# One decode-and-prompt step of a hybrid trunk: every fp32 tile at an offset of a table, in another order of the same steps

## The chip, the cores and the metric

The kernel runs on one core of one Trainium2 chip. The metric is the time of one execution on the device, in microseconds. The core's engines are TensorE (PE; its weight loads are shown apart as PEld), VectorE (DVE), ScalarE (ACT), GpSimd (POOL) and SyncE (SP). SP, ACT and POOL also issue transfers between HBM and the on-chip memory.

## The reference

One layer of a trunk with two branches side by side, run on a prompt of 512 tokens and on 8 sequences that each add one token to a past of 4,096.

```python
mod = silu(c) @ w_ada + b_ada;  shift, scale, gate = split(mod, 3)
h = rmsnorm(x, g_norm) * (1 + scale) + shift
q, k, v, z_att, fl, u, z_ssm = split(h @ w_in)     # 512 each, fl: 8
logf = log_sigmoid(fl + b_fgate)
# attention, 8 heads of 64: scores get the sum of logf between the key and the query
#   prompt: causal over 512;  samples: 4096 past rows through page_table, and the new one
# state-space branch: 32 groups of 16 channels, 64 complex states each
#   h_t = a_bar * h_{t-1} + b_bar u_t;  y = Re(C h) + d_skip * u
att = o_att * silu(z_att)
g = gelu(y);  ssm = g * sigmoid(g @ w_glu + b_glu) * silu(z_ssm)
y = x + gate * (concat(att, ssm) @ w_out)          # then a final rmsnorm
```

All is fp32. The outputs are y for prompt and samples, the new k, v and logf, and the last states. The cache that the samples read is 8 x 4096 rows of k and as many of v, 512 values a row: 134 MB, by far the largest part of what is read.

## The kernel before

**Steps and order.** The kernel is written as a program that records. `Engine` wraps each engine, and every call on it (`V.` for DVE, `A.` for ACT, `P.` for POOL, `PE.`, `SP.`) adds one step to a list in `Steps`. There are 2,881 steps; a step can hold several matrix products that go side by side on TensorE (`join`). At the end `issue()` goes through a table `ORDER` of 2,881 step numbers and issues the steps in that order, so that the table fixes the order on each engine's queue. Waits between engines follow from which memory a step reads and writes. All instructions of the profile are therefore issued in one line, L245, and are told apart by their tiles.

**The decode part.** `decode()` walks through 64 blocks of K and 64 of V: 8 for each of 8 sequences. `issue(n)` takes a buffer of 128 x 2048 fp32 (1.05 MB) from `kvt()` and fills it by an indirect gather from POOL's queue, 8 KB a partition. `dec_k(n)` multiplies half of a K block by the query on POOL and half on DVE, and sums over the head dimension, a quarter on ACT (32 short instructions) and the rest by a reduction on DVE. `dec_soft(b)` makes the softmax of a sequence. `dec_v(n)` multiplies a V block on TensorE into the PSUM tile `pv`.

**The prompt part.** `prompt()` holds the rest: the state-space branch `ssm_phase()`, the projections, `attn()` over four pairs of heads and four blocks of 128 queries, the gates, the output projection. Before both, in the body of the function, come the adaLN products, the transposed input `hT`, and the tables of the state-space part, which are a long chain of small DVE steps. The weights come in tiles of 1 MB from SP's queue (`wload`, `w`, `qk`).

**Memory.** Small constants, `hT` and the like have a pool of their own (`cp`). Other tiles come from rings: `wp` has 3 buffers of 1 MB, `qkp` 2, `kva` 3, and `sm` 2 of each name. Two arenas, `arA` (12,864 fp32 a partition) and `arB` (12,640), are single tiles in which `Arena` hands out fixed ranges by name; the memory of the early tables in `arA` is used again later under other names. A cache block has one of five buffers, three of the ring `kva` and two in `arA`:

```python
def kvt():
    n = kvp[0]
    kvp[0] += 1
    if kvp[1] is not None and n % 5 in (1, 2):
        return kvp[1].tile([128, 2048], F32, name="kv", bufs=2)
    return kva.tile([128, 2048], F32, name="kv")
```

PSUM's eight banks are rings too: three for products (`mm`), two for transposes (`tr`), and one each for `sm`, `pv` and `q`.

In the profile `kv` is a buffer of the ring and `arA` can be a cache block, a table or anything else of that arena.

Of the kernel before, what the change touches and what calls it, by code (L numbers as in the profile page):

```python
# [21 lines left out]
B = 8  # L22
# [10 lines left out]
AK = 50.25  # L33
BK = 49.375
# [24 lines left out]
ORDER = [  # L59
# [1462 lines left out]
```

## Time and profile before

| what | value |
|---|---|
| median of three runs | 576.67 us (571.11 to 577.95) |
| profiled execution | 576.52 us, span 574.5 us |
| mean granted TensorE clock | 0.948 |
| moved | 176.50 MB, mean 307 GB/s |
| of this, gathers from POOL (queue q0) | 135.74 MB |
| PE busy | 471.2 us, 82% of the span |
| DVE busy | 405.3 us, 71% |
| POOL busy | 315.4 us, 55% |
| ACT busy | 288.4 us, 50% |

The span goes from the first instruction to the last. A busy share is that of an engine over the span or a part of it; PE's is modelled and is not a share of its peak. The row of the transfers gives the mean busy share of 16 transfer engines. A row of waits reads: who waited, for whom, us in total, how often, the longest. A row of a group reads: line, engine, operation, what is written from what, count, busy us, mean ns of one, and the idle time before them with what ended it. A row of the chain reads: start, us, what.

### The profile page before, as it was taken

Reading aid. Unit: us, or ns where it says so; the run is one execution under the profiler, and the core shown is the slowest. Engines: PE = TensorE matmul, PEld = TensorE weight load, DVE = VectorE, ACT = ScalarE, POOL = GpSimd, SP = SyncE. Lnnn points to the kernel's source line nnn. Section 1 sums busy time; section 2 is a strip of 40 time slices with the busy share of each in tenths; the row PEclk is TensorE's granted clock in tenths of the full one; section 3 lists DMA queues with packets and bytes.
Section 4 is the critical chain, followed back from the end, with each engine's and each line's share of the span. In section 5 each row is a group of like instructions: output and inputs, shape, how many; then the busy total and the mean of one; then the engine's idle time right before and its main releaser. Section 6 shows DMA issues by size and latency. Waiting matters only on the chain.

```text
span 574.5 us, 9192 instructions
## 1 busy us (share of the span) xinstructions
PE 471.2 (82%) x3158; PEld 227.6 (40%) x3158; DVE 405.3 (71%) x712; ACT 288.4 (50%) x1353; POOL 315.4 (55%) x239
## 2 busy tenths in 40 slices
PE   1847795899798987789997988789789799989984
PEld 1315384455343435455532332333234343433331
DVE  6998999989988776455586466676664662765535
ACT  4344252435236834616354895687874782532211
POOL 6157174445168757665636566547845664536431
PEclk9969899799799999999998998999899889999998
DMA  8979544564498999999998898999999899699883
GB/s 252 385 259 290 193 150 147 192 251 136 158 338 334 339 354 356 335 357 370 329 372 295 318 354 315 411 374 327 352 364 362 317 371 413 246 374 349 344 359 149
DMA packets 45335, 176.50 MB, mean 307 GB/s; under 512 B 6981, under 2 KB 21737, under 8 KB 27881
## 3 DMA queue, kind: packets, MB, share of 16 engines
q0 software_dynamic: 19264, 135.74, 63.1%
q1 hardware_dynamic: 25376, 39.40, 19.6%
q10 hardware_dynamic: 648, 0.78, 0.4%
q8 instruction: 25, 0.41, 0.3%
q14 instruction: 22, 0.17, 0.1%
HBM read 171.48 MB, written 4.42 MB: 306 GB/s over the span
## 4 chain that ended last, share of the span: by engine, by line
DMA 35%; DVE 18%; PE 13%; issue 11%; POOL 8%; ACT 5%; POOLq 0%; DVEq 0%; ACTq 0%
DMA kv<-in_cache_k_dram,kidx 16%; PE mm L245 9%; DMA kv<-in_cache_v_dram,kidx 7%; DVE arA L245 6%; DMA arA<-in_cache_v_dram,kidx 6%; POOL kv L245 5%; DVE sc L245 5%; DMA arA<-in_cache_k_dram,kidx 4%; PE pv L245 3%; DVE kv L245 3%; POOL arA L245 3%; ACT arB L245 2%; DVE arB L245 2%; ACT kv L245 1%; DVE hT L245 1%
## 5 line engine op out<-in xcount | busy, mean ns | idle before, releaser
L245 PE MATMUL mm<-hT,w 128*128 128x512 f32 x256 | 130.1, 631 | 1.3 <-PE pv L245 0.6
L245 ACT ACTIVATE kv<-kv 128x64 f32<-128x64 f32 x304 | 73.7, 244 | 68.0 <-DVE kv L245 58.7
L245 POOL TENSOR_TENSOR kv<-kv,qs 128x1024 f32<-128x1024 f32 x38 | 89.7, 2363 | 30.7 <-DMA kv<-in_cache_k_dram,kidx 29.7
L245 ACT ACTIVATE arA<-arA 128x64 f32<-128x64 f32 (+1 forms) x215 | 52.4, 246 | 50.4 <-DVE arA L245 47.9
L245 POOL TENSOR_TENSOR arA<-arA,qs 128x1024 f32<-128x1024 f32 x26 | 61.6, 2369 | 28.1 <-DMA arA<-in_cache_k_dram,kidx 22.4
L245 DVE TENSOR_TENSOR kv<-kv,q 128x1024 f32<-128x1024 f32 x38 | 46.0, 1213 | 35.0 <-DMA kv<-in_cache_k_dram,kidx 28.1
L245 POOL DMA_INDIRECT kv<-in_cache_k_dram,kidx x38 | 37.6, 988 | 58.7 <-PE pv L245 13.3
L245 DVE TENSOR_REDUCE sc<-kv 128x24 f32<-128x1536 f32 x38 | 66.2, 1743 | 3.6 <-POOL kv L245 3.4
L245 PEld LDWEIGHTS mm<-hT,w 128*128 128x128 f32 x256 | 45.7, 198 | 47.6 <-issue 42.9
L245 POOL DMA_INDIRECT kv<-in_cache_v_dram,kidx x38 | 37.7, 992 | 42.3 <-PE pv L245 20.2
L245 ACT ACTIVATION_READ_ACCUMULATOR kv<-kv 128x1 f32 x304 | 57.5, 189 | 0.0
L245 DVE TENSOR_TENSOR arA<-arA,q 128x1024 f32<-128x1024 f32 x26 | 31.5, 1213 | 34.9 <-DMA arA<-in_cache_k_dram,kidx 31.3
L245 PE MATMUL pv<-kv,arA 128*32 128x512 f32 x304 | 42.0, 630 | 16.9 <-DMA kv<-in_cache_v_dram,kidx 16.5
L245 DVE TENSOR_REDUCE sc<-arA 128x24 f32<-128x1536 f32 x26 | 45.4, 1745 | 6.1 <-POOL arA L245 5.9
L245 DVE TENSOR_TENSOR arA<-arA 128x512 f32<-128x512 f32 (+9 forms) x105 | 45.2, 452 | 0.8
L245 POOL DMA_INDIRECT arA<-in_cache_k_dram,kidx x26 | 25.2, 969 | 37.4 <-PE pv L245 25.5
L245 ACT ACTIVATION_READ_ACCUMULATOR arA<-arA 128x1 f32 x208 | 39.4, 189 | 0.0
L245 PE MATMUL mm<-qk,hT 128*64 128x256 f32 x256 | 32.9, 419 | 7.2 <-ACT arA L245 7.0
L245 PE MATMUL pv<-arA 128*32 128x512 f32 x208 | 28.5, 623 | 11.2 <-DMA arA<-in_cache_v_dram,kidx 8.3
L245 POOL DMA_INDIRECT arA<-in_cache_v_dram,kidx x26 | 25.3, 975 | 18.6 <-ACT arA L245 7.6
L245 ACT ACT_TABLE_LOAD x25 | 32.1, 1283 | 4.3 <-PEq L1504 1.7
L245 PEld LDWEIGHTS mm<-qk,hT 128*64 128x64 f32 x256 | 26.1, 201 | 12.9 <-ACT arA L245 7.4
(245 smaller groups left out, 835.1 us busy)
## 6 DMA issues: line engine op xcount, KB each, us to landing
w<-in_w_in_dram SPq DMA_DIRECT2D x10, 1024.0 KB
w<-in_w_ada_dram SPq DMA_DIRECT2D x9, 1024.0 KB
kv<-in_x_prompt_dram SPq DMA_DIRECT2D x2, 1024.0 KB
qk<-in_w_ada_dram SPq DMA_DIRECT2D x2, 1024.0 KB
qk<-in_w_in_dram SPq DMA_DIRECT2D x2, 1024.0 KB
qk<-in_w_out_dram SPq DMA_DIRECT2D x2, 1024.0 KB
w<-in_w_out_dram SPq DMA_DIRECT2D x2, 1024.0 KB
hT<-in_x_prompt_dram SPq DMA_DIRECT2D x1, 2048.0 KB
```

What stands on the lines that cost most here:

```text
L245: fn(*args, **kw)
```

## The change

The rings and arenas go. There is one block, `heap`, of 51,712 fp32 a partition, and eight PSUM tiles, one for each bank. A second table, `PLACE`, has one entry for each of the 671 fp32 and PSUM tiles in the order in which the program asks for them: an offset in the block, or a bank. Tiles of other types (bf16 and int32) get memory of their own. `ORDER` is another permutation of the same 2,881 step numbers. `kvt()` no longer has five buffers but a place from the table for each of the 128 blocks. The table `Toep`, which lay over the memory of `slotB`, gets an entry of its own.

```diff
-AK = 50.25
-BK = 49.375
+HEAP = 51712
+ORDER = [
+    201, 336, 50, 22, 21, 4, 112, 39, 64, 23, 24, 43, 37, 38, 42, 484, 135, 11, 276, 1, 25, 202, 41, 5, 3, 182,
...
-ORDER = [
-    4, 337, 1711, 25, 23, 24, 242, 1, 202, 3, 201, 50, 484, 336, 21, 22, 60, 64, 39, 112, 41, 6, 243, 11, 61,
...
-class Ring:
-    def __init__(self, pool, bufs):
-        self.pool, self.bufs = pool, bufs
-
-    def tile(self, shape, dtype, name, bufs=None):
-        return self.pool.tile(shape, dtype, name=name, bufs=bufs or self.bufs)
...
+    def tile(self, shape, name, psum=False):
+        at, w = PLACE[self.n], int(np.prod(shape[1:]))
+        self.n += 1
+        v = self.banks[at][:shape[0], 0:w] if psum else self.heap[:shape[0], at:at + w]
...
-class Arena:
...
-    cp, sm, wp, qkp, kva = (ring(n, b) for n, b in (("consts", 1), ("small", 2), ("w", 3), ("qk", 2), ("kva", 3)))
-    ps = ring("ps", 1, space=PSUM)
-    ar = ctx.enter_context(tc.tile_pool(name="arenas", bufs=1))
-    arA = ar.tile([128, int(AK * 256)], F32, name="arA")
-    arB = ar.tile([128, int(BK * 256)], F32, name="arB")
...
+    heap = cp.tile([128, HEAP], F32, name="heap")
+    banks = [pp.tile([128, 512], F32, name=f"bank{i}") for i in range(8)]
...
+    class Room:
+        def tile(self, shape, dtype, name, bufs=1, room=0):
+            return T_(shape, name) if dtype == F32 else fixed(shape, dtype, name + str(steps.n))
+
+    cp_, sm, wp, qkp, kva, sa, tb, tp = (Room() for _ in range(8))
+
+    mmt = trt = tbt = smt = bank
...
     def kvt():
         n = kvp[0]
         kvp[0] += 1
-        if kvp[1] is not None and n % 5 in (1, 2):
-            return kvp[1].tile([128, 2048], F32, name="kv", bufs=2)
         return kva.tile([128, 2048], F32, name="kv")
...
-        o = tp.names["slotB0"][0]
-        Toep = arB[:, o:o + 4096].rearrange("p (a j x) -> p a j x", a=2, j=4)
+        Toep = T_([128, 2, 4, 512], "Toep")
...
         if b % 4 == 0 and c == 0:
-            pv_t[0] = ps.tile([128, 512], F32, name="pv", bufs=1)
+            pv_t[0] = bank()
```

More of the change, by code (lines that the diff above doesn't have):

```diff
@@ L32 @@
 PRE = 1
-AK = 50.25
-BK = 49.375
+HEAP = 51712
+ORDER = [
[151 rows of a table added]
+PLACE = [
[36 rows of a table added]
 XAT = 5
@@ L53, with __init__, own, add @@
 NEG = -1e30
-ORDER = [
[151 rows of a table removed]
-]
 class Engine:
     def __init__(self, steps, name, eng):
-        self._s, self._e = steps, eng
+        self._s, self._n, self._e = steps, name, eng
     def __getattr__(self, method):
-        return lambda *args, join=False, **kw: self._s.add(getattr(self._e, method), args, kw, join)
-class Ring:
-    def __init__(self, pool, bufs):
-        self.pool, self.bufs = pool, bufs
-    def tile(self, shape, dtype, name, bufs=None):
-        return self.pool.tile(shape, dtype, name=name, bufs=bufs or self.bufs)
-class Steps:
-    def __init__(self):
-        self.ops = []
-    def add(self, fn, args, kw, join):
+        return lambda *args, join=False, **kw: self._s.add(self._n, method, getattr(self._e, method), args, kw, join)
+class Steps:
+    def __init__(self, nc, heap, banks):
+        self.ops, self.heap, self.banks, self.n = [], heap, banks, 0
+    def tile(self, shape, name, psum=False):
+        at, w = PLACE[self.n], int(np.prod(shape[1:]))
+        self.n += 1
+        v = self.banks[at][:shape[0], 0:w] if psum else self.heap[:shape[0], at:at + w]
+        if len(shape) > 2:
+            ax = "abcd"[:len(shape) - 1]
+            v = v.rearrange(f"p ({' '.join(ax)}) -> p {' '.join(ax)}", **dict(zip(ax, shape[1:])))
+        return v
+    def own(self, t):
+        return t
+    def add(self, eng, method, fn, args, kw, join):
         if join:
@@ L245, in issue @@
                 fn(*args, **kw)
-class Arena:
-    def __init__(self, t, start=0):
-        self.t, self.at, self.names = t, start, {}
-    def tile(self, shape, dtype, name, bufs=1, room=0):
-        n = max(room, int(np.prod(shape[1:])))
-        if name not in self.names:
-            self.names[name] = [self.at, n, bufs, 0]
-            self.at += n * bufs
-            assert self.at <= self.t.shape[1], (name, self.at)
-        e = self.names[name]
-        assert n <= e[1], name
-        o = e[0] + e[1] * (e[3] % e[2])
-        v = self.t[:shape[0], o:o + int(np.prod(shape[1:]))]
-        e[3] += 1
-        if len(shape) > 2:
-            ax = "abcd"[:len(shape) - 1]
-            v = v.rearrange(f"p ({' '.join(ax)}) -> p {' '.join(ax)}", **dict(zip(ax, shape[1:])))
-        return v
 def dap(t, off, dims):
@@ L281, in tile_fox_s5_step, with T_, bank, fixed @@
     ctx.enter_context(tc.manual_schedule())
-    plan = Steps()
-    V, A, P, PE, SP = (Engine(plan, n, e) for n, e in (("DVE", nc.vector), ("ACT", nc.scalar), ("Pool", nc.gpsimd),
-                                                       ("PE", nc.tensor), ("SP", nc.sync)))
-    def ring(name, bufs, **k):
-        return Ring(ctx.enter_context(tc.tile_pool(name=name, bufs=bufs, **k)), bufs)
-    cp, sm, wp, qkp, kva = (ring(n, b) for n, b in (("consts", 1), ("small", 2), ("w", 3), ("qk", 2), ("kva", 3)))
-    ps = ring("ps", 1, space=PSUM)
-    ar = ctx.enter_context(tc.tile_pool(name="arenas", bufs=1))
-    arA = ar.tile([128, int(AK * 256)], F32, name="arA")
-    arB = ar.tile([128, int(BK * 256)], F32, name="arB")
-    sa = tb = Arena(arA)
-    tp = Arena(arB)
-    def mmt():
-        return ps.tile([128, 512], F32, name="mm", bufs=3)
-    def trt():
-        return ps.tile([128, 512], F32, name="tr", bufs=2)
-    tbn = [0]
-    def tbt():
-        tbn[0] += 1
-        return ps.tile([128, 512], F32, name=("sm", "pv")[tbn[0] % 2], bufs=1)
-    def smt():
-        return ps.tile([128, 512], F32, name="sm", bufs=1)
+    cp = ctx.enter_context(tc.tile_pool(name="consts", bufs=1))
+    pp = ctx.enter_context(tc.tile_pool(name="banks", bufs=1, space=PSUM))
+    heap = cp.tile([128, HEAP], F32, name="heap")
+    banks = [pp.tile([128, 512], F32, name=f"bank{i}") for i in range(8)]
+    steps = Steps(nc, heap, banks)
+    V, A, P, PE, SP = (Engine(steps, n, e) for n, e in (("DVE", nc.vector), ("ACT", nc.scalar), ("Pool", nc.gpsimd),
+                                                        ("PE", nc.tensor), ("SP", nc.sync)))
+    def T_(shape, name):
+        return steps.tile(shape, name)
+    def bank():
+        return steps.tile([128, 512], "bank", psum=True)
+    def fixed(shape, dtype, name):
+        return steps.own(cp.tile(shape, dtype, name=name))
+    class Room:
[3 more added lines that the diff above has]
+    mmt = trt = tbt = smt = bank
     def mm(out, lhsT, rhs, start=True, stop=True, **k):
@@ L365, in tile_fox_s5_step @@
         wada.append(t)
-    pt_i = cp.tile([NPG, B], I32, name="pt_i")
+    pt_i = cp_.tile([NPG, B], I32, name="pt_i")
     P.dma_start(pt_i, dap(page_table, 0, [[1, NPG], [NPG, B]]))
-    ident = cp.tile([128, 128], F32, name="ident")
+    ident = cp_.tile([128, 128], F32, name="ident")
     pcol = sa.tile([128, 1], F32, name="pcol")
     P.iota(pcol, pattern=[[1, 1]], base=0, channel_multiplier=1, allow_small_or_imprecise_dtypes=True)
-    ones = cp.tile([128, 128], F32, name="ones")
+    ones = cp_.tile([128, 128], F32, name="ones")
     V.memset(ones, 1.0)
@@ L379, in tile_fox_s5_step @@
         bns.append(bn)
-    bfr = cp.tile([8, 8], F32, name="bfr")
+    bfr = cp_.tile([8, 8], F32, name="bfr")
     P.dma_start(bfr, dap(b_fgate, 0, [[0, 8], [1, 8]]))
-    bfc = cp.tile([8, 1], F32, name="bfc")
+    bfc = cp_.tile([8, 1], F32, name="bfc")
     P.dma_start(bfc, dap(b_fgate, 0, [[1, 8], [1, 1]]))
@@ L393, in tile_fox_s5_step @@
     P.affine_select(tri, ones, pattern=[[-1, 128]], compare_op=OP.is_gt, fill=0.0, base=0, channel_multiplier=1)
-    identb = cp.tile([128, 128], BF16, name="identb")
+    identb = cp_.tile([128, 128], BF16, name="identb")
     V.tensor_copy(identb, ident)
-    maskb = cp.tile([128, 128], BF16, name="maskb")
+    maskb = cp_.tile([128, 128], BF16, name="maskb")
     P.memset(maskb, 0.0)
     P.affine_select(maskb, maskb, pattern=[[-1, 128]], compare_op=OP.is_ge, fill=NEG, base=0, channel_multiplier=1)
-    nhalf = cp.tile([128, 8], F32, name="nhalf")
+    nhalf = cp_.tile([128, 8], F32, name="nhalf")
     V.memset(nhalf, -0.5)
-    s4 = cp.tile([128, 32], F32, name="s4")
+    s4 = cp_.tile([128, 32], F32, name="s4")
     V.tensor_reduce(s4, ident.rearrange("p (q x) -> p x q", x=32), axis=AX.X, op=OP.add)
-    m8c = cp.tile([128, 8], F32, name="m8c")
+    m8c = cp_.tile([128, 8], F32, name="m8c")
     V.tensor_reduce(m8c, ident.rearrange("p (q h) -> p h q", h=8), axis=AX.X, op=OP.add)
-    oh = cp.tile([128, 2, 8], F32, name="oh")
+    oh = cp_.tile([128, 2, 8], F32, name="oh")
     V.memset(oh, 0.0)
@@ L415, in tile_fox_s5_step @@
     PE.transpose(t[:, 128:192], xs64, ident[:64, :64])
-    cs = cp.tile([128, 8, 32], F32, name="cs")
+    cs = cp_.tile([128, 8, 32], F32, name="cs")
     V.memset(cs, 0.0)
     A.activation(cs[:, :, 0:9], t[:, 0:72].rearrange("p (r k) -> p k r", k=8), AF.Silu)
-    gcol = cp.tile([128, 12], F32, name="gcol")
+    gcol = cp_.tile([128, 12], F32, name="gcol")
     V.tensor_copy(gcol, t[:, 72:84])
@@ L459, in tile_fox_s5_step @@
     V.tensor_scalar(rowf, pg4[:, :B], pm, None, op0=OP.add)
-    lidx = cp.tile([128, B], I32, name="lidx")
+    lidx = cp_.tile([128, B], I32, name="lidx")
     V.tensor_copy(lidx, rowf)
-    kidx = cp.tile([128, B, 8], I32, name="kidx")
+    kidx = cp_.tile([128, B, 8], I32, name="kidx")
     for c in range(8):
@@ L472, in gather @@
                                     in_offset=bass.IndirectOffsetOnAxis(ap=idx, axis=0))
-    suf = cp.tile([128, B, 33, H], F32, name="suf")
+    suf = cp_.tile([128, B, 33, H], F32, name="suf")
     for b in range(B):
         gather(suf[:, b, 0:32].rearrange("p s h -> p (s h)"), lrows, lidx[:, b:b + 1])
-    hT = cp.tile([128, 8, S], F32, name="hT")
+    hT = cp_.tile([128, 8, S], F32, name="hT")
     ssx = tb.tile([128, 4], F32, name="ssx")
@@ L509, in tile_fox_s5_step @@
     V.scalar_tensor_tensor(Am, Am, 1.0, gcol[:, 0:8, None].to_broadcast([128, 8, 9]), op0=OP.add, op1=OP.mult)
-    hTs = cp.tile([128, 8, 32], F32, name="hTs")
+    hTs = cp_.tile([128, 8, 32], F32, name="hTs")
     V.memset(hTs, 0.0)
@@ L547, in svec @@
     def svec(name, pool=None):
-        return (pool or cp).tile([8, 512], F32, name=name)
-    xq = cp.tile([128, 512], F32, name="q_s")
+        return (pool or cp_).tile([8, 512], F32, name=name)
+    xq = cp_.tile([128, 512], F32, name="q_s")
     xs2 = xq[:, 0:256]
@@ L557, in tile_fox_s5_step @@
             acopy(q_s[:, c], t, scale=HD ** -0.5)
-    s4b = cp.tile([128, 32], BF16, name="s4b")
+    s4b = cp_.tile([128, 32], BF16, name="s4b")
     V.tensor_copy(s4b, s4)
-    qsp = cp.tile([72, 512], BF16, name="qsp")
+    qsp = cp_.tile([72, 512], BF16, name="qsp")
     V.memset(qsp, 0.0)
@@ L797, in dec_q @@
     def dec_q(b):
-        dq = ps.tile([128, 512], F32, name="q", bufs=1)
+        dq = bank()
         mm(dq, s4b[:72, b:b + 1].to_broadcast([72, 128]), qsp)
@@ L826, in tile_fox_s5_step @@
     V.tensor_copy(xf[:, 0:32], t[:, 0:32])
-    lf = cp.tile([128, 40], F32, name="lf")
+    lf = cp_.tile([128, 40], F32, name="lf")
     z1 = tb.tile([128, 40], F32, name="z1")
@@ L856, in suffix @@
             V.tensor_tensor(suf[:, :, s], suf[:, :, s], suf[:, :, s + 1], op=OP.add)
-    mT = cp.tile([8, 8], F32, name="mT")
-    sn = cp.tile([8, 8], F32, name="sn")
-    den = cp.tile([128, B, H], F32, name="den")
+    mT = cp_.tile([8, 8], F32, name="mT")
+    sn = cp_.tile([8, 8], F32, name="sn")
+    den = cp_.tile([128, B, H], F32, name="den")
     pv_t = [None]
@@ L1057, in attn @@
         attT = res["attT"]
-        spare = Arena(arA, kvp[1].names["gr"][0])
-        cum = spare.tile([8, S], F32, name="cum")
+        cum = T_([8, S], "cum")
         t = trt()
@@ L1063, in attn @@
         V.tensor_tensor_scan(cum, ones[:8, 0:1].to_broadcast([8, S]), t[:8], 0.0, op0=OP.mult, op1=OP.subtract)
-        ncs = cp.tile([72, S], BF16, name="ncs")
+        ncs = cp_.tile([72, S], BF16, name="ncs")
         V.memset(ncs, 0.0)
@@ L1267, in sample_kv @@
             A.dma_start(xs2[32 * j:32 * j + 8], dap(x_sample, 256 * j, [[D, 8], [1, 256]]))
-    late = Arena(arA)
+    late = Room()
     kvp[1] = m8p[0] = m8p[1] = late
@@ L1299, in prompt @@
         yield from fill
-        rp = ap = Arena(arB)
+        rp = ap = Room()
         v_sv, za_s = u_s, y_sv
@@ L1391, in prompt @@
         drain(at)
-        ap = Arena(arB, rp.names["PT0"][0])
         wo = []
@@ L1458, in tile_fox_s5_step @@
         next(gp)
-    acc, steps = 0, 0
+    acc, turns = 0, 0
     while True:
-        acc += R1 if steps < N1 else RATE
-        steps += 1
+        acc += R1 if turns < N1 else RATE
+        turns += 1
         while acc >= 1:
@@ L1489, in tile_fox_s5_step @@
         (SP, A)[j % 2].dma_start(dap(y_s, 256 * j, [[D, 8], [1, 256]]), xs2[32 * j:32 * j + 8])
-    plan.issue()
+    steps.issue()
 _INS = ["x_prompt", "x_sample", "c_prompt", "c_sample", "cache_k", "cache_v", "cache_logf",
```

336 rows, old and new, of tables (ORDER, PLACE) are left out of this document.

## The prediction

> **What bounds the kernel now.** The page's totals come first, then its strip of 40 slices, then the same strip cut into four stages.
>
> ```profile
> span 574.5 us, 9192 instructions
> PE 471.2 (82%) x3158; PEld 227.6 (40%) x3158; DVE 405.3 (71%) x712; ACT 288.4 (50%) x1353; POOL 315.4 (55%) x239
> ...
> DMA  8979544564498999999998898999999899699883
> ...
> q0 software_dynamic: 19264, 135.74, 63.1%
> q1 hardware_dynamic: 25376, 39.40, 19.6%
> ```
>
> No engine is full over the span. The strip shows two regimes: transfers at 4 to 6 tenths from the fifth to the eleventh slice, then 8 to 9 tenths nearly to the end. q0 carries the gathers of the cache, 128 of 1.05 MB (8 KB in each of 128 partitions), and they are most of the traffic.
>
> ```profile
> core 0: us, PE busy (x) PEld busy (x) DVE busy (x) ACT busy (x) POOL busy (x), PEclk, DMA share, GB/s
> 0.00:57.40 57.40, 30.32 (x282) 15.92 (x283) 49.76 (x164) 23.32 (x37) 30.14 (x34) 0.91 0.89 297
> 57.40:172.30 114.90, 98.24 (x784) 57.93 (x788) 109.19 (x236) 44.89 (x251) 52.47 (x35) 0.91 0.55 195
> 172.30:545.70 373.40, 323.58 (x1969) 146.39 (x1962) 233.30 (x286) 216.18 (x1057) 225.82 (x159) 0.97 0.93 347
> 545.70:574.50 28.80, 19.02 (x133) 7.40 (x131) 13.05 (x28) 4.05 (x9) 6.92 (x12) 0.92 0.63 254
> ```
>
> In the first stage the weights come in and transfers are nearly full. In the second, DVE is busy for 109.19 of 114.90 us (the tables of the state-space part and the first score products) and the transfers are idle for 45% of the time, 52 us. In the third, 373.40 us long, transfers are at 0.93 and every engine has room: DVE 140 us, PE 49.8, POOL 147.6. The last is the end of the work, where little is left to move.
>
> The chain that ended last says what the third stage waits for.
>
> ```profile
> DMA 35%; DVE 18%; PE 13%; issue 11%; POOL 8%; ACT 5%; POOLq 0%; DVEq 0%; ACTq 0%
> ```
> ```profile
> 182.38 1.22 issue
> 183.60 7.56 DMA kv<-in_cache_k_dram,kidx
> 191.30 2.36 POOL kv L245
> 193.66 0.89 POOL arA L245
> 194.54 1.85 issue
> 196.62 1.04 POOL kv L245
> 197.96 7.49 DMA kv<-in_cache_k_dram,kidx
> 205.59 2.35 POOL kv L245
> ```
>
> This is a loop through POOL's queue. A gather takes some 7.5 us to land; a product on POOL (2.36 us) waits for it; only when that is done does POOL come to its next gather, and the loop starts again. The waits of the third stage tell the same from both sides.
>
> ```profile
> POOL kv L245 <- DMA kv<-in_cache_k_dram,kidx: 29.7, 16, 5.4
> POOL kv L245 <- PE pv L245: 26.0, 11, 4.6
> POOL arA L245 <- DMA arA<-in_cache_k_dram,kidx: 16.8, 8, 4.5
> POOL arA L245 <- PE pv L245: 16.6, 11, 3.7
> POOL kv L245 <- ACT kv L245: 13.4, 9, 4.2
> ...
> POOL arA L245 <- ACT arA L245: 7.6, 4, 3.9
> ```
> ```profile
> PE pv L245 <- DMA kv<-in_cache_v_dram,kidx: 16.5, 11, 3.9
> ...
> PE pv L245 <- DMA arA<-in_cache_v_dram,kidx: 6.8, 8, 1.7
> ```
>
> POOL's products wait 46.5 us for transfers; its gathers wait 63.6 us (35 times, 1.8 us each) until PE or ACT has finished with the buffer that they will fill. PE waits 23.3 us for V blocks. So the third stage is bound by the **transfers, at a depth that five buffers allow**: 7% of 373 us, 26 us, are idle although data is wanted.
>
> **The change, part by part.**
>
> *Allocators replaced.* Both ORDER tables hold the same 2,881 step numbers, so no instruction is added or taken and shapes stay. The classes that go run at build time: 0 us, with no bound on either side, since nothing of them is executed. One count should change. ACT loads a table whenever the function that follows needs another one, 1.28 us each:
>
> ```profile
> L245 ACT ACT_TABLE_LOAD x25 | 32.1, 1283 | 4.3 <-PEq L1504 1.7 <-DVE arB L245 0.7 <-DMA arA<-in_b_glu_dram 0.6
> ```
>
> Leaving out Copy, Identity and Square, the old order changes function 24 times on ACT, which with the first load is the 25 of the row; the new order changes it 21 times. Three loads less are 3.9 us of ACT, at 50% over the span, so I count 0; with that cover gone it would be -4.
>
> *Room for the gathers.* Before, a gather fills one of five buffers. In the new tables I set each gather's place in ORDER against the place of the last step that reads its block, and count the blocks that are issued and not yet finished. Over gathers 1 to 20 their mean goes from 3.9 to 5.1, over 21 to 38 from 4.0 to 5.3, over 39 to 72 from 4.0 to 8.4, over 73 to 92 from 4.4 to 6.4, over 93 to 128 from 4.1 to 9.5; the most from 5 to 12. In POOL's queue alone, a product had on average 2.4 younger gathers ahead of it, and now has 4.1; those with none or one fall from 15 of 64 to 11. While POOL waits for a block, that many more are under way.
>
> *Third stage.* It moved 347 GB/s x 373.4 us = 129.6 MB; at a share of 0.93 that is 373 GB/s when busy. Bounds: a share that stays at 0.93 gives 0 us, a share of 1.00 gives 129.6 MB / 373 GB/s = 347 us, -26 us. I take 0.97, nearer to the full end since the depth doubles, but not full, since 27 of the 128 gathers stand within five places after the last reader of their memory and so still wait on POOL: 129.6 / 362 = 358 us, **-15 us**. The other engines allow it: PE would be busy 324 of 358 us, and its 23.3 us of waits for V blocks are of the kind that goes. What is late next is PE.
>
> The Trainium skill has a rule against this, in "DMA: Bandwidth & Descriptors", section "Where 436 GB/s comes from": between HBM and SBUF a core is held to about 358 GB/s. By it the stage could not go below 362 us, -11 us in place of -15. Its 358 GB/s was passed by the 28.7 us window at 459.60 that is quoted under the rivals.
>
> *Second stage.* The tables have the same DVE work ahead of the scores: the 40th block is finished with 240 us of DVE work queued before it in the old order and 246 in the new (each instruction's own duration in this trace, overlap included, summed in the order of the table). So DVE stays the bound there and no work leaves it. The gathers come sooner: ahead of gather 16, 20, 24, 28, 32, 36 DVE has 173, 184, 198, 205, 219, 224 us of work before, 155, 176, 186, 202, 210, 218 after, 9 us less on average; PE has 173, 186, 206, 212, 237, 247 before, 166, 183, 202, 213, 229, 244 after, 4 us less. A lead of the gathers moves the transfer-bound stage forward by as much. Bounds: -9 us by DVE, and +5 us if the earlier gathers hold up the weights that come on the other queue (u's two loads now have 6 to 8 us of PE work ahead of their first use, before 24 to 32). I take PE's end, since both engines are needed: **-5 us** (4 and a little for DVE).
>
> *First stage and end.* The first gather moves from behind 29 us of POOL work to behind 16, but transfers are at 0.89 there: 0 beyond the lead just counted. The last gather has 614 us of PE work ahead of it before and 610 after, 429 of DVE in both: 0 at the end.
>
> *PSUM by table.* Eight banks serve all uses in place of 3+2+1+1+1. Counting a new bank's use that comes within 1 us of PE work after the bank's last reader, there are 56 of 203 before and 61 after: 0 us. Bounds: 5 more waits of at most 2.5 us (the longest that PE's transposes waited in the row below) are +12, and -8 is that row gone.
>
> ```profile
> PE tr L245 <- ACT arB L245: 7.9, 9, 2.5
> ```
>
> **Sum.** The profiled execution took 576.5 us, its span 574.5, so 2.0 lie around the span; the median of the three runs is 576.7 (571.1 to 578.0), the same. 576.5 - 15 - 5 = **556 us**, 3.5% less. About 2% is what a measurement of this kernel tells from no change.
>
> **Rivals.**
>
> *The memory is at its ceiling.* Three windows of the third stage, by start and end, with clock, share and GB/s last:
>
> ```profile
> 201.00:229.80 28.80, 22.85 (x241) 12.63 (x240) 20.14 (x27) 11.94 (x63) 18.57 (x15) 1.00 0.96 354
> ...
> 373.40:402.10 28.70, 25.35 (x129) 10.98 (x128) 19.50 (x28) 22.75 (x113) 17.06 (x13) 1.00 0.97 350
> ...
> 459.60:488.30 28.70, 27.36 (x128) 12.17 (x125) 13.07 (x18) 15.37 (x54) 14.72 (x10) 0.94 1.01 392
> ```
>
> Shares of 0.96 and 0.97 moved 354 and 350 GB/s, hardly more than the stage's mean: more transfers in flight might only make each slower. Then 129.6 MB / 354 = 366 us, -7, and with PE holding the second stage nothing more: 569 us, no change. For it: those two windows. Against it: the 392 of the third. Chance 0.25. With the Trainium skill's 358 GB/s ("DMA: Bandwidth & Descriptors", the same section) for the 354, this rival would give 565 us.
>
> *POOL's queue becomes the bound (slower).* Of the 128 gathers, 36 now fill memory whose last user was not a cache block: 16 weight tiles, 8 of the softmax, 12 others. If the projection or attention step in question is late, POOL stands, with every product behind it on its queue, DVE's reduction waits for the product, the softmax for that, and PE for the softmax. POOL has 147.6 us idle in the third stage; 15 go with the shorter stage and 63.6 are the release waits of before, so 69 are left for new ones: from 1.9 us for each of the 36 it costs time. Seen were 1.8 us on average and 4.6 at most. At 2.5 us it is 90 us, 21 over what fits; with the third stage's gain lost and the lead of 5 kept, 576.5 + 21 - 5 = 593 us. For it: waits on PE are the largest release waits already. Against it: deeper buffers let the waiting gather be one that nobody needs soon. Chance 0.12.
>
> *It doesn't do what it says.* If accesses to the one block were ordered as if they were all to the same place, gathers could not overlap and 128 of 7.5 us alone would be 960 us. Against it: buffers in the old arena block arA and other arA work did run side by side. Chance 0.02.
>
> **How the numbers follow.** Chances: forecast 0.57 (541 to 565), ceiling 0.25 (565 to 582), POOL 0.12, not as said 0.02, and 0.04 that it goes below its bounds. The predicted time is the likeliest case's, 556. The range takes the bounds of the terms: 576.5 - 26 - 9 - 4 = 538 at the low end, 576.5 + 5 = 582 at the high end, the second stage's worst with no gain. PSUM's two ends are not added, since all ends do not fall together. The range leaves out the slower cases and little else, under 0.2. Faster by over 2% (below 565): 0.61. Within 2%: 0.26. Slower: 0.13.
>
> **What the changed profile would show.** If the steps are right: stage three's share at 0.96 or more with 360 GB/s or more; PE's waits for V blocks well under 23 us and POOL's products' waits under 46; the second stage still with DVE at 95%, and transfers there at 0.58 to 0.62; 22 table loads; in the chain fewer alternations of a gather and a POOL product. A share that rises with GB/s at 350 is the ceiling; gathers on POOL that wait over 100 us for PE and ACT with transfers below 0.93 is the slower rival. The forecast is wrong too if the second stage moves by more than 9 us, which I hold DVE's work to forbid.

## The result and the profile after

| kernel | median, us | range, runs |
|---|---|---|
| before | 577.31 | 571.11 to 580.14, 4 |
| changed | 545.70 | 543.36 to 549.00, 4 |

The ratio is 0.9491, with an interval of 0.9389 to 0.9592: **faster by 5.1%**. The profiled execution took 547.14 us, 29.4 less than that of before. Each ratio in this document compares fast runs of a kernel with fast runs of before from the same session, so it is not always the quotient of the medians beside it, and the profiled executions of runs 3, 10, 11 and 12 are slow ones, 0.9 to 1.4% above their medians.

From the page of the changed kernel, its head, the totals of the engines, the strip of transfers in 40 slices and the two large transfer queues:

```profile
span 545.2 us, 9185 instructions
PE 463.1 (85%) x3158; PEld 228.4 (42%) x3158; DVE 404.2 (74%) x712; ACT 282.6 (52%) x1350; POOL 308.3 (57%) x239
...
DMA  8997904363898999999999999989999999998984
...
q0 software_dynamic: 19264, 135.74, 64.8%
q1 hardware_dynamic: 25376, 39.40, 21.0%
```

The same work and the same bytes in 29 us less. The strip still has its thin part, from the sixth to the tenth slice, but from the twelfth on it is nearly all 9. The table by stage (columns as before) has the first two cuts where they were; the last one is put 28.8 us before the end, as it was.

```profile
0.00:57.40 57.40, 31.38 (x301) 17.79 (x301) 51.37 (x165) 24.00 (x38) 21.13 (x33) 0.97 0.90 306
57.40:172.30 114.90, 97.86 (x806) 58.63 (x807) 109.94 (x229) 46.67 (x276) 63.23 (x42) 0.93 0.60 212
172.30:516.40 344.10, 315.46 (x1858) 143.72 (x1860) 226.77 (x283) 204.98 (x1020) 216.45 (x153) 0.97 0.97 368
516.40:545.20 28.80, 18.40 (x200) 8.29 (x192) 16.14 (x37) 6.91 (x16) 7.46 (x13) 0.94 0.70 279
```

All of the difference lies between 172.3 us and the last stage, which is 29.3 us shorter, but it has two sources. Up to 172.3 us the changed kernel has moved 306 x 57.4 + 212 x 114.9 = 41.9 MB, against 39.5 before: work that the long stage no longer has. The last stage moves some 0.7 MB more as well (279 against 254 GB/s). And the long stage itself moves 368 GB/s where it moved 347. PE stands still for 28.6 us of it, before for 49.8.

Who waited in that stage, by engine (who, for whom, us, times, longest):

```profile
PE bank L280 <- ACT heap L280: 15.5, 18, 2.9
PE bank L280 <- DVE heap L280: 7.7, 6, 2.7
PE bank L280 <- DMA heap<-in_cache_v_dram,kidx: 4.9, 4, 2.4
```
```profile
POOL heap L280 <- PE bank L280: 52.6, 28, 7.2
POOL heap L280 <- ACT heap L280: 27.0, 18, 4.6
POOL heap L280 <- DMA heap<-in_cache_k_dram,kidx: 20.8, 5, 6.1
```

PE's wait for V blocks went from 23.3 to 4.9 us; what is left of PE's waits are the small ones for ACT and DVE. POOL's waits for K blocks went from 46.5 to 20.8. DVE's wait for K blocks, before and then after, over the whole span:

```profile
DVE arA L245 <- DMA arA<-in_cache_k_dram,kidx: 31.3, 12, 5.8
...
DVE kv L245 <- DMA kv<-in_cache_k_dram,kidx: 28.1, 19, 4.2
```
```profile
DVE heap L280 <- DMA heap<-in_cache_k_dram,kidx: 20.5, 8, 4.7
```

59.4 us became 20.5. What did not change is POOL's own standing at its gathers. The groups of gathers (busy us, mean ns, then idle time before them and what ended it):

```profile
L245 POOL DMA_INDIRECT kv<-in_cache_v_dram,kidx x38 | 37.7, 992 | 42.3 <-PE pv L245 20.2 <-ACT kv L245 15.1 <-issue 4.1
L245 POOL DMA_INDIRECT kv<-in_cache_k_dram,kidx x38 | 37.6, 988 | 58.7 <-PE pv L245 13.3 <-issue 13.1 <-ACT kv L245 12.8
L245 POOL DMA_INDIRECT arA<-in_cache_v_dram,kidx x26 | 25.3, 975 | 18.6 <-ACT arA L245 7.6 <-issue 3.6 <-DVE arB L245 2.7
L245 POOL DMA_INDIRECT arA<-in_cache_k_dram,kidx x26 | 25.2, 969 | 37.4 <-PE pv L245 25.5 <-DVE arA L245 5.0 <-issue 4.2
```
```profile
L280 POOL DMA_INDIRECT heap<-in_cache_k_dram,kidx x64 | 63.5, 992 | 81.0 <-PE bank L280 27.1 <-ACT heap L280 25.1 <-DVE heap L280 13.7
L280 POOL DMA_INDIRECT heap<-in_cache_v_dram,kidx x64 | 63.2, 987 | 72.1 <-PE bank L280 31.7 <-ACT heap L280 23.4 <-issue 10.4
```

Before 157.0 us in sum, after 153.1. POOL still stops at a gather until its memory is free; what it loads comes earlier for those who need it.

### The profile page after: what moved, and what is told of

Same layout as the page of the kernel before. It is cut to its first block, busy times and chain, and to the rows that moved or that the text cites. A ratio compares the mean times of both kernels' runs of the same rounds, so it can differ in the third digit from the quotient of the medians.

```text
span 545.2 us, 9185 instructions
## 1 busy us (share of the span) xinstructions
PE 463.1 (85%) x3158; PEld 228.4 (42%) x3158; DVE 404.2 (74%) x712; ACT 282.6 (52%) x1350; POOL 308.3 (57%) x239
## 5 line engine op out<-in xcount | busy, mean ns | idle before, releaser
L280 PE MATMUL bank<-heap 128*32 128x64 f32 (+15 forms) x3086 | 456.9, 410 | 71.3 <-DVE heap L280 29.2
L280 PEld LDWEIGHTS bank<-heap 128*32 128x32 f32 (+7 forms) x3086 | 222.8, 142 | 294.7 <-issue 173.3
L280 ACT ACTIVATE heap<-heap 128x64 f32<-128x64 f32 (+4 forms) x595 | 171.3, 295 | 137.2 <-DVE heap L280 116.2
L280 POOL TENSOR_TENSOR heap<-heap 128x1024 f32<-128x1024 f32 (+2 forms) x71 | 156.2, 2208 | 33.7 <-DMA heap<-in_cache_k_dram,kidx 31.0
L280 DVE TENSOR_REDUCE heap<-heap 128x24 f32<-128x1536 f32 (+5 forms) x88 | 126.6, 1449 | 18.8 <-POOL heap L280 17.3
L280 DVE TENSOR_TENSOR heap<-heap 128x512 f32<-128x512 f32 (+9 forms) x263 | 115.1, 470 | 5.0 <-ACT heap L280 2.6
L280 DVE TENSOR_TENSOR heap<-heap,bank 128x1024 f32<-128x1024 f32 (+3 forms) x82 | 83.1, 1029 | 45.5 <-DMA heap<-in_cache_k_dram,kidx 20.5
L280 POOL DMA_INDIRECT heap<-in_cache_k_dram,kidx x64 | 63.5, 992 | 81.0 <-PE bank L280 27.1
L280 POOL DMA_INDIRECT heap<-in_cache_v_dram,kidx x64 | 63.2, 987 | 72.1 <-PE bank L280 31.7
L280 ACT ACTIVATION_READ_ACCUMULATOR heap<-heap 128x1 f32 x521 | 98.5, 189 | 0.0
L280 ACT ACT_TABLE_LOAD x22 | 28.2, 1283 | 11.8 <-DVE heap L280 9.3
```

Of the source, the lines that this page charges most:

```text
L280: fn(*args, **kw)
```

## Experiments

The theory at the start was that of the prediction: the gathers stand further ahead of their use ("lead", counted in steps of the order between the gather and the first step that reads its block: 32 on average before, 57 after), and that carries the gain. The rivals: the new order of all other steps, and the block with its places. In the diffs below one entry of a table stands for all; G marks the gather. Times are read from the medians and the ratios, and from the profiles only what is larger than 1.4%. "POOL's idle time at its gathers" is the sum of the idle times in front of the two groups of gathers, over the whole span: 157.0 us before, 153.1 in the changed kernel.

**1. Old order in the block.**

```diff
-ORDER = [201, 336, 50, 22, 21, 4, ...   # new
+ORDER = [4, 337, 1711, 25, 23, 24, ...  # old
-PLACE = [...]                           # the change's
+PLACE = [...]                           # packed tightly for the old order
```


> The old order of steps, with its fp32 tiles at table offsets in the new block (five fixed places for the gathered cache blocks, as before) and the PSUM banks in the old groups of 3, 2, 1, 1 and 1. The output is the reference's. Theory (the gain comes from where the gathers stand in the order): within 2% of the kernel before, 577 us (566 to 588). Rival A (the other steps' new order carries the gain): the same 577, since no step is moved. Rival B (the block itself carries it: dependencies followed by exact range in place of ring buffers, so that fewer false waits are left): at most 562 us.

Measured: 611.95 us (605.44 to 619.19), ratio to before 1.0524 (1.0441 to 1.0606). None of the cases has that: no step was moved, and 35 us were lost.

**2. Old order, gathers earlier.** 102 gathers moved, 56 blocks at another place.

```diff
 ORDER around place 1800
-  1914, 1862, G1754, 1865, 1872
+  1805, 1863, G1754, 1864, 1913         # 14 places earlier
```


> The old order, with the 128 gathers alone moved earlier, each to a mean of 57 steps before its block's first use, which is the new order's mean (32 in the old one); no other step is moved. Theory: most of the gain comes with it, 545 to 560 us. Rival A (the order of the other steps): 568 to 588, no measurable change. A third case, that gathers put early in the old order block the queue of POOL while its products wait behind them: above 590.

Measured: 631.62 us (624.24 to 633.88), ratio 1.0971 (1.0911 to 1.1031). That is the time of the third case, and POOL's idle time at its gathers is 215.6 us here, in run 1 185.8. The run does not show the third case alone: PE's wait for w_in rose as well, from 11.0 us in run 1 to 24.1, with 56 blocks at other places.

**3. New order, gathers later.** 98 gathers moved, no place changed.

```diff
-  1750, 2020, G1766, 1886, 2019
+  1961, 1887, G1766, 1888, 1381         # 32 places later
```


> The new order and its table of places, with the gathers alone moved later, none more than 30 steps ahead of its block's first use (mean lead 30.5 steps against 57 in the new order and 32 in the old). Theory: most of the gain is lost, 562 to 578 us. Rival A: 543 to 553, the gain stays with the order of the other steps.

Measured: 585.77 us (581.19 to 590.78), ratio 1.0124 (1.0045 to 1.0203). The whole gain is lost, and 8 us more. The two longer stages of this run, the second of them taken to its own last gathers:

```profile
57.40:172.30 114.90, 91.60 (x792) 57.01 (x780) 104.99 (x216) 42.83 (x255) 58.80 (x38) 0.93 0.53 199
172.30:558.00 385.70, 338.84 (x1972) 153.12 (x1975) 242.75 (x317) 210.14 (x1046) 225.58 (x161) 0.93 0.89 338
```

Transfers fall back from 212 to 199 and from 368 to 338 GB/s. Everything but the gathers' positions is as in the changed kernel, so these positions are **necessary** for the gain.

**4. New order, gathers earlier still.** 86 gathers moved, 9 blocks at another place.

```diff
-  1871, 1781, G1778, 1733, 1727
+  1658, 1835, G1778, 1915, 1836         # 16 places earlier
```


> The new order, with the gathers moved earlier still where the block has room, to a mean lead of 69 steps (57 in the new order). Theory: a little more of the same, 536 to 545 us, since the transfers' share of 0.97 in the last stage leaves little and only the stretch before 172 us (share 0.60) has room. Rival A: 543 to 550, no change. Against both: POOL waits in its queue at gathers whose places are not free yet, above 555.

Measured: 566.54 us (564.82 to 569.04), ratio 0.9832 (0.9773 to 0.9890). More lead is worse by 21 us than the changed kernel. The gathers of this run:

```profile
L278 POOL DMA_INDIRECT heap<-in_cache_k_dram,kidx x64 | 65.1, 1017 | 79.5 <-PE bank L278 38.3 <-DVE heap L278 13.7 <-issue 13.3
L278 POOL DMA_INDIRECT heap<-in_cache_v_dram,kidx x64 | 62.7, 980 | 102.6 <-PE bank L278 58.9 <-ACT heap L278 28.9 <-issue 11.8
```

A gather put ahead of the step that frees its memory waits at the head of POOL's queue, with the products behind it: 182.1 us of idle time at the gathers against 153.1, and the wait for PE ahead of V's gathers is 58.9 us where it was 31.7. That is the prediction's slower rival, and it sets in a short way beyond the change's own order. "More lead is more gain" had fallen.

**5. Old order, rested places.** The places of the first run again, chosen so that a tile lies where the last user was done long ago.

```diff
 PLACE, entries 16 and 17 (two weight tiles)
-  0, 2048
+  2288, 192
```


> The old order again, the old groups of PSUM banks, no step moved; the places in the block are chosen so that a tile is put where the last user was done long before, by the times of the old trace (in the first run with the old order they were packed without regard to that, and it took 612 us). Theory P (what that run lost, it lost to places reused too soon): 566 to 588 us, as before. Rival A (the old order cannot live with exact ranges in one block, wherever the tiles lie): at least 600. Rival B (places alone carry the gain of the change, once they are good): at most 560.

Measured: 622.72 us (618.49 to 627.36), ratio 1.0689 (1.0578 to 1.0801). Theory P's time did not come: places rested by the times of the old trace were no better than packed ones. The waits of this run show what it loses instead (PE's first, then one of DVE's):

```profile
PE bank L278 <- DMA heap<-in_w_in_dram: 23.6, 3, 16.0
...
PE bank L278 <- DMA heap<-in_w_out_dram: 12.3, 2, 8.0
DVE heap L278 <- DMA heap<-in_x_prompt_dram: 12.1, 1, 12.1
```

None of the three rows exists before. These are loads on SP's queue, and they are issued later: the four of w_out at 493.8 to 532.0 us, spread over 38 us, where the kernel before issues them at 460.3 to 468.3, within 8. (Run 1 has 11.0 us at w_in, 7.9 at w_out and 20.0 at w_ada.)

**6. Old order, early gathers, rested places.** Run 5 with 99 gathers moved and 281 tiles at other places.

```diff
-  1914, 1862, G1754, 1865, 1872
+  1659, 1730, G1754, 1909, 1802         # 39 places earlier
```


> The old order with the gathers alone moved earlier, to a mean of 56 steps before first use as in the new order (32 in the old), and places chosen for long rest as in the run before. Theory (lead of the gathers carries the gain, and the first try was spoiled by its places): at most 562 us. Rival A (the order of the other steps carries it): within 8 us of the old order with rested places. Third case (an early gather blocks POOL's queue until its place is free): at least 15 us above the old order with rested places.

Measured: 620.44 us (616.53 to 623.43), ratio 1.0669 (1.0589 to 1.0749). Within 8 us of run 5, as rival A had it, but PE waits 17.7 us for w_out here, so the run decides little.

**7. New order, fresh places.** The order, the banks and the cache blocks' places are the change's.

```diff
 PLACE, entry 25 (a weight tile)
-  24576
+  22528
```


> The new order and its PSUM banks, the cache blocks at the change's places; of the other fp32 tiles 226 are put elsewhere, each where the last user was done latest. Theory P (rest of a place counts): at least 565 us. Rival (the order alone carries it, places have room to spare): 543 to 553.

Measured: 579.40 us (575.80 to 583.62), ratio 1.0002 (0.9968 to 1.0036). Moving 226 tiles, without a step of the order, takes **all** of the gain, as theory P had it. POOL's idle time at its gathers is 197.4 us here (113.9 and 83.5), 44 more than in the changed kernel, and PE waits 17.4 us for w_ada in place of 11.8. Which of the 226 tiles make it so was not separated.

**8. New order, rested places.**

```diff
 PLACE, entries 15, 29, 30 (early tables), 50 (a bank)
-  48384, 45824, 44800, 6
+  32320, 30273, 29249, 7
```


> The new order unchanged, with 277 tiles (36 of them cache blocks) put at places that had rested longer by the times of the trace of the changed kernel. Theory P: 535 to 543 us. Rival (the change's own places already cost nothing that ends last): 543 to 553.

Measured: 538.91 us (534.68 to 542.74), ratio 0.9232 (0.9134 to 0.9329). **It beats both kernels**, as theory P had it; its interval lies below that of the change. The two were compared through the runs of before in their own sessions, not side by side. The 277 tiles include 12 banks, so it is not shown that places in the block alone carry this gain. Its long stage is as full as the change's. It is cut 11 us sooner here, since its 19th gather is issued at 147.5 us and that of the changed kernel at 157.5:

```profile
57.40:161.00 103.60, 95.64 (x824) 58.17 (x817) 100.13 (x225) 45.94 (x273) 62.80 (x42) 0.98 0.64 232
161.00:508.00 347.00, 319.68 (x1866) 145.03 (x1865) 225.84 (x285) 205.88 (x1025) 216.22 (x154) 0.96 0.96 367
```

**9. Old order, old layout written as places.** Of the wide tiles, all but 41 lie where their ring or arena had them.

```diff
 PLACE, entries 16 and 17 (two weight tiles), against run 1
-  0, 2048
+  33760, 35808
```


> The old order in the new block, this time with the old layout written as places: every weight, cache block and other tile of 300 elements or more where its ring or arena had it (e2, qs, q_s and slotB3, 41 tiles of 512 or 1024, excepted), the small ones between them, the old groups of PSUM banks. By the old trace no weight load and no gather has to wait longer for its place than it did. Theory Q (the first two runs with the old order lost their time at the weight loads, whose places came free late: PE waited 8 to 24 us for w_in and 8 to 18 us for w_out, which it never did before): 568 to 586 us, as the kernel before. Rival A (the old order cannot live with exact ranges in one block): at least 600. Rival B (the block carries the gain): at most 562.

Measured: 592.12 us (586.30 to 594.62), ratio 1.0175 (1.0063 to 1.0287). The rows for w_in and w_out are gone, and with them 20 of run 1's 35 us: theory Q for the larger part. Some 13 us stay. So the block by itself gives no gain; whether the 13 us are a cost of its own or that of the places that differ from the old layout is open. About half of them can be placed: the stage from 57.4 to 172.3 us moves 173 GB/s here in place of 195, and its 19th gather is issued at 174.7 us, in the kernel before at 167.0.

**10. The same with early gathers.** 107 gathers moved, 45 blocks at other places that no weight load waits for.

```diff
-  1781, 1866, G1736, 1755, 1756
+  1805, 1863, G1736, 1864, 1913         # 20 places earlier
```


> The run before with the gathers alone moved earlier, to a mean of 55 steps before first use (32 in the old order, 57 in the new), 45 cache blocks of 128 put where the old layout has free room for it, and no place taken that a weight load waits for. Theory (the gathers' lead, with places for it, carries the gain): 545 to 565 us. Rival A (the order of the other steps is needed too): within 8 us of the run before. Third case (early gathers hold up POOL's queue): 10 us or more above the run before.

Measured: 587.50 us (584.87 to 594.26), ratio 1.0103 (1.0004 to 1.0203). That is rival A's case, within 5 us of run 9, and the two intervals overlap. Its waits, with nearly the whole of the new order's lead (55 of 57 steps):

```profile
DVE heap L277 <- DMA heap<-in_cache_k_dram,kidx: 37.1, 16, 8.5
...
PE bank L277 <- DMA heap<-in_cache_v_dram,kidx: 32.0, 13, 5.7
```

The waits for K blocks are shorter (on DVE 37.1 us in place of 68.8, on POOL 12.5 in place of 49.4), and the time is hardly less. PE's wait for V blocks is as long as in run 9 (30.8). So the lead alone, in the old order and with these places, is **not sufficient**. That K blocks are not what counts does not follow. POOL's waits from 172.3 us on, of run 9 and then of this run:

```profile
POOL heap L277 <- PE bank L277: 56.7, 30, 8.3
POOL heap L277 <- DMA heap<-in_cache_k_dram,kidx: 42.8, 18, 5.2
POOL heap L277 <- ACT heap L277: 33.9, 16, 10.8
```
```profile
POOL heap L277 <- PE bank L277: 88.3, 25, 11.3
POOL heap L277 <- ACT heap L277: 44.2, 18, 11.0
...
POOL heap L277 <- DMA heap<-in_cache_k_dram,kidx: 3.9, 5, 1.8
```

The three rows add up to 133.4 us and to 136.4: what POOL no longer waits for K blocks, it waits for memory to come free. The idle time at its gathers rose from 179.4 to 216.4 us, which is the sign of the third case. Shorter waits for K blocks with a free queue were not tried in the old order.

**11. New order, the first 24 gathers late.** 16 of them had to move.

```diff
-  381, 917, G979, 744, 577
+  384, 386, G979, 904, 778              # 25 places later
```


> The new order and its places, the first 24 gathers alone moved later, to at most 30 steps before first use (a mean of 29 against 59); the other 104 stay. With all 128 late it took 586 us, 40 more than the changed kernel. Theory (the lead of the early stretch is worth what the traces show between gather 1 and gather 24, 8 to 10 us, and the rest falls after it): 550 to 558 us. Rival A (what is lost early is made up by the later gathers, which are bounded by something else): 543 to 549. Rival B (the early lead is all of it, later gathers live off it): at least 570.

Measured: 553.37 us (552.26 to 561.23), ratio 0.9540 (0.9446 to 0.9633). By the medians the early lead is worth 7.7 us, as the theory had it; by the ratios it is 0.5%, 3 us, and the intervals of this run and of the changed kernel overlap. Either way it is small against run 3's 40 us, so most of that loss lies in the later gathers.

**12. New order, V's gathers late.** 52 moved, all of V blocks.

```diff
-  2022, 1991, G1878, 1940, 1992
+  2094, 2095, G1878, 2096, 1820         # 52 places later
```


> The new order and its places, with the 64 gathers of V blocks alone moved later, to at most 30 steps before first use (a mean of 32 against 58); the 64 of K blocks stay. With all 128 late it took 586 us, 40 above the changed kernel. Theory V (what ends last in the long stage is TensorE's wait for V blocks: 23 us of it before, 5 after, 25 with all late; the K blocks' waits on VectorE and GpSimd have cover): 568 to 590 us, TensorE's waits for V blocks in that stage back above 15 us. Rival K (the wait for K blocks on VectorE and GpSimd is what counts; it fell by 65 us with the change): 546 to 556.

Measured: 577.90 us (569.98 to 584.42), ratio 0.9891 (0.9840 to 0.9942). Of run 3's loss in ratio against the change (1.0124 - 0.9491 = 0.063) V's gathers alone make 0.040. PE's and POOL's waits in the stage from 172.3 to 552 us of this run, and the stage:

```profile
PE bank L278 <- DMA heap<-in_cache_v_dram,kidx: 24.7, 10, 4.8
```
```profile
POOL heap L278 <- DMA heap<-in_cache_k_dram,kidx: 21.7, 6, 5.7
```
```profile
172.30:552.00 379.70, 332.90 (x1949) 150.86 (x1947) 237.64 (x307) 208.52 (x1039) 220.39 (x158) 0.94 0.90 338
```

POOL's wait for K is what it is in the changed kernel (20.8); PE's wait for V is back at 24.7, and the rate of the transfers has fallen below the old 347 GB/s. Both signs of theory V came: the time, and PE's waits above 15 us. Two other waits rose too, so PE's is not shown to be the only one that counts. POOL's idle time at its gathers is 178.9 us, nearly that of run 4, and DVE's wait for K blocks went from 20.5 to 33.0. Run 3 speaks against POOL's standing as the cause, since it loses 40 us with 142.0 us of it. The counterpart, K's gathers late alone, was not run. (The 25 us "with all late" of the expectation is that of the whole span; from 172.3 us on it is 18.3 in run 3.)

## Why the prediction was right, and where it was not

The forecast was 556 us, the time is 545.7: the direction and the stage were right, the gain was 32 us instead of 20. The reason given for it was right in part, as the points below say.

- **Third stage, -15.** The share went to 0.97, just as taken. The stage had 368 x 344.1 = 126.6 MB left to move. At the old 347 GB/s they take 365 us, at 347 x 0.97/0.93 = 362 GB/s 350 us, which is the 15 of the forecast. But the rate while busy, held at 373 GB/s, became 368/0.97 = 379, which makes the 350 us 344: 6 more. The term measured -21.
- **Second stage, -5.** DVE stayed the bound (109.94 of 114.90 us, 96%) and transfers stood at 0.60, as forecast. What is left of the 29.3 us is the lead, 29.3 - 21 = 8 us; of it, 2.4 MB more moved by 172.3 us are 2.4/347 = 7. Of the two ends it was DVE's 9 that came near, not PE's 4. Run 11 gives 3 to 8 us from the other side, which is too coarse to tell the two ends apart.
- **The depth behind it.** The argument said that while POOL waits, that many more gathers are under way. Hardly more are: counted from the issue of each gather to the end of its last packet, there were on average 2.00 under way in the third stage before and 2.11 after, with 2.08 in run 10 and 2.05 in run 12. The 5% more go with the 6% more that the stage moved a second; the depth in the tables had doubled. The extra room is filled otherwise.
- **Where the room went.** From the first to the last instruction on it (a mean of the 64 in the trace), a K block was in use for 15.2 us on average before, and 26.9 in the changed kernel; in run 10 for 16.7. A V block was issued 10.0 us before its use and now 14.6, in run 12 12.2. So the new room goes into K blocks that lie longer between their product and the end of their sums on ACT (eight sums a block, not the 32 instructions of the opening), and into V blocks that are issued earlier. The second is not the whole account, since run 10 has 13.9 us for V blocks, and PE waits 32.0 us there. Run 10 also lacks the depth: counted as in the prediction, its unfinished blocks are 4.5 to 6.0 on average in the five stretches and 8 at most, against 5.1 to 9.5 and 12 in the new order. Run 3 has K blocks in use for 28.3 us and no gain, so the longer use without the lead does not do it either. Which of the other moved steps are needed was not separated.
- **"PE's 23.3 us of waits are of the kind that goes".** They did (4.9 us left), and run 12 brings back most of the loss together with them. Whether the chain's loop through POOL and K blocks was the wrong half is open: run 10 cuts the waits for K blocks, but POOL then stands as long at its gathers.
- **Allocators replaced, 0 with no bound.** This step of the prediction failed. It priced the classes that run at build time and not the places. With the order untouched, other places made +34 us (run 7) and, with 12 banks moved too, -7 (run 8) by the medians, +29 and -15 by the ratios; with the old order they cost 35 to 45 (runs 1 and 5). That the forecast came near is luck in this respect: it left the places out, and this table's are good ones. Why run 9 still loses 13 us is open; 41 wide tiles and the small ones lie otherwise there than in the rings.
- **PSUM by table, 0.** It was not tried by itself; run 8 moved 12 banks among other tiles.
- **The ceiling.** The rival at 354 GB/s is out: the stage moved 368 over 344 us. The Trainium skill's limit of about 358 GB/s ("DMA: Bandwidth & Descriptors", section "Where 436 GB/s comes from") would make its 126.6 MB take 354 us at least; the trace has 344.1, and the measurement decides.
- **The slower rival** is real but was not reached. Run 4 shows it, 21 us above the changed kernel with 29 us more of idle time at POOL's gathers; in run 2, 20 us above run 1, PE's wait for w_in is mixed in.
- **Details.** There are 22 table loads, as counted. That the chain would show fewer alternations can't be read: it goes back over a quarter of the span only (the shares of the second row below add up to 27%).

```profile
L280 ACT ACT_TABLE_LOAD x22 | 28.2, 1283 | 11.8 <-DVE heap L280 9.3
...
PE 17%; DVE 3%; DMA 2%; issue 2%; ACT 2%; POOL 1%; POOLq 0%; DVEq 0%; ACTq 0%
```

What it does reach is PE: the engine that was to be late next.

## What to carry to other kernels

A table of places is a schedule of its own: a place decides when the next load into it may start, and a load that waits holds up what stands behind it on its queue (POOL stood 182.1 us at its gathers in run 4), so price every moved tile by when its last reader ends against when its next load wants to begin. A gather's position has an optimum, since too late starves the reader and too early stops the queue that issues it; they cost 40 and 21 us here (runs 3 and 4). When an edit shortens one wait, look on the same queue for the wait that took its place before you call the first one harmless.

## What was not expected of the hardware

The same 3,158 matrix instructions took longer in the profiles with a lower mean clock. Spans and mean granted clock of the changed kernel, of run 7 and of run 5, and PE's busy time in runs 7 and 5:

```profile
core 0: 545.2 us, clock 0.956
```
```profile
core 0: 581.9 us, clock 0.931
...
PE 477.1 (82%) x3158; PEld 233.5 (40%) x3158; DVE 404.7 (70%) x712; ACT 283.2 (49%) x1350; POOL 308.2 (53%) x239
```
```profile
core 0: 624.8 us, clock 0.902
...
PE 486.5 (78%) x3158; PEld 234.3 (37%) x3158; DVE 407.1 (65%) x712; ACT 287.6 (46%) x1353; POOL 314.5 (50%) x239
```

PE was busy for 463.1, 477.1 and 486.5 us: with 37 us more of span between the first two came 14 us more of busy time. Busy time multiplied by the mean clock gives 443, 444 and 439 us, nearly the same, so the longer busy time goes with the lower clock. The clock is lower where PE stands longer, 82, 105 and 138 us of the span; that the waits lower it is a reading of three profiles and was not tested. The Trainium skill says, in "TensorE: Matmul & The Clock Gate", section "HAM oscillation — how this bites in real kernels", that gaps of PE above some 3.4 us should be avoided. The rows agree in direction: the longest wait of PE's products for a V block is 2.4 us in the changed kernel and 4.8 in run 12, at clocks of 0.97 and 0.94 in that stage. But the stage of before has a longest such wait of 3.9 us and a clock of 0.97 too. A threshold they don't show.
